# A depthwise convolution of 31 taps: 17 taps as band matrices over four tokens x 32 channels on TensorE, 14 taps on VectorE

## The chip, the cores and the metric

The kernel runs on one core of a Trainium2 chip. The metric is the device time of one execution in microseconds (us). A core has five engines that each work through an instruction list of their own, in order: TensorE (PE in the profile; its weight loads are shown apart, as PEld), VectorE (DVE), ScalarE (ACT), GpSimd (POOL) and SyncE (SP), which here only issues DMA transfers. They meet at semaphores. Matmuls read SBUF and write PSUM; DVE and ACT reach both memories.

## What is computed

The model has two layers on 512 tokens of width 1024: a mixer with a feed-forward part, then a conformer convolution with a feed-forward part. The change lies in the conformer:

```python
def conformer_conv(t, w1, b1, dw_w, dw_b, ln_g, ln_b, w2, b2):
    a, gate = jnp.split(t @ w1 + b1, 2, axis=-1)
    u = dwconv1d(a * jax.nn.sigmoid(gate), dw_w, dw_b)
    u = jax.nn.silu(layer_norm(u, ln_g, ln_b))
    return u @ w2 + b2
```

`dwconv1d` is a convolution along the tokens, each channel with its own 31 weights: out[t] is the sum over d from -15 to 15 of w[d] u[t+d], with zeros outside. All in float32.

## The kernel before

Data lies with channels on the 128 partitions and the 512 tokens along the free axis, so the 1024 channels are eight blocks `i` of 128. Every product in float32 is made of three matmuls: both factors are split into a rounded high part and the rest (type fp32r), and `mm3w` (lines 214 to 216) issues high x high, high x low and low x high into one PSUM tile. The projections `ps` of `cw1` and `cw2` go that way, 8 x 3 matmuls of 512 columns for one block of output. Weights come by DMA as `wraw`, ACT casts them to `whi`, POOL or DVE subtracts to `wlo` (`_wload`).

The conformer works through the blocks in four pairs, `ip` = 0, 2, 4, 6. For each block PE projects gate and value, ACT takes the sigmoid `sg` (line 1128), and DVE makes `u` (line 1133), which lies in PSUM for blocks 0 to 5 and in SBUF for 6 and 7. `split` (lines 985 and 986) gives `uhi` on ACT and `ulo` on DVE. The convolution is then shared out:

- ACT does the centre tap and the bias into the accumulator `cr` (line 1146).
- PE does 10, 10, 12 and 20 taps per block in the four pairs (`PE_TAPS`), each as a product with a diagonal matrix: `diag` scales the identity by the 128 weights on ACT, once for the high and once for the low part (lines 1109 and 1110, 208 instructions in all), and `mm3w` sums into `pc`. A tap is a shifted slice of `uhi` and `ulo`.
- DVE does the others, 20, 20, 18 and 10 per block, one fused multiply-add each over all tokens (`ve`, line 1163), by turns on the accumulators of the two blocks of the pair.

`add` brings both together on DVE (line 1168) and adds to the sums for the layer norm, `a1` and `a2` (`ln_add`, lines 929 to 931: a square on ACT, two additions, on POOL for the first three pairs and on DVE for the last). The last pair is done in two halves of 256 tokens. `stats_later` hangs two callbacks into `mm3w` that fire after a count of products: the first sums over partitions on PE (`sm`, line 945) and runs 15 tiny DVE operations to the mean `st` and the inverse deviation `rs`; the second spreads these on PE (`pb`, line 961) and starts `normed`, which is 24 DVE operations a half (lines 966, 967 and 986) with the Silu on ACT (line 1116) between them. Then `group("cw2")` projects (`psg`), the first half of the tokens first; `flush` in it fires the callbacks that are still open.

A scheduler orders each engine's list by the program's order and its own view of when things are ready; waits come from the tiles' dependencies.

Of the kernel before, what the change touches and what calls it, by code (L numbers as in the profile page):

```python
# [147 lines left out]
class Net:  # L148
# [62 lines left out]
    def mm3w(self, ps, w, a, start, stop):  # L211
# [4 lines left out]
        mm(ps, w[1], a[0], start=False, stop=stop)  # L216
# [870 lines left out]
    def conformer(self):  # L1087
        nc = self.nc
        PAD = 16
# [13 lines left out]
        kept = {}

        def diag(i, tap, bufs=4):
            wc = slice(tap * 8 + i, tap * 8 + i + 1)
            dhi = ct.tile([P, P], F32R, tag=f"dhi{bufs}", name="dhi", bufs=bufs)
            dlo = ct.tile([P, P], F32R, tag=f"dlo{bufs}", name="dlo", bufs=bufs)
            nc.scalar.mul(dhi, self.ident, whi[:, wc].bitcast(F32))
            nc.scalar.mul(dlo, self.ident, wlo[:, wc].bitcast(F32))  # L1110
            return dhi, dlo
# [10 lines left out]
        for ip in range(0, KT, 2):  # L1122
            us = []
            for i in (ip, ip + 1):
                pg = nxt(D + i * P)
                pa = nxt(i * P)
                sg = self.work.tile([P, T], F32, tag="t", name="sg")
                nc.scalar.activation(out=sg, in_=pg, func=AF.Sigmoid, bias=self.pc("cb1", 8 + i))
# [4 lines left out]
                nc.vector.scalar_tensor_tensor(out=u, in0=pa, scalar=self.pc("cb1", i), in1=sg, op0=ALU.add, op1=ALU.mult)
# [8 lines left out]
            pet = self.PE_TAPS[ip // 2]
            mid = KC // 2
            pcs = [self.mm.tile([P, T], F32, tag="mm", name="pc") for _ in us]
            for i, (u, _, _) in zip((ip, ip + 1), us):
                nc.scalar.activation(out=cr[:, i, :], in_=u, func=AF.Identity, scale=self.pc("cdw", mid * 8 + i), bias=self.pc("cdb", i))  # L1146
# [108 lines left out]
```

## Time and profile before

| | |
|---|---|
| median of 3 runs | 1750.29 us (1748.7 to 1751.08) |
| profiled execution | 1750.37 us, span 1748.6 us |
| conformer's convolution, first `pc` to first normalise operation of the second half | 1163.17 to 1316.91 |

The page gives the engines' busy time as a share of the span, and the chain of work that ended last. Rows of a timeline give start, duration, engine, line, operation and output <- inputs, with shapes; idle time of the engine ahead of a row stands in brackets with what ended it. Durations of matmuls overlap: what one costs is the step from start to start.

### The profile page before, as it was taken

What the parts mean: (1) busy time and instruction counts of PE and PEld (TensorE: products, weight loads), DVE (VectorE), ACT (ScalarE), POOL (GpSimd) and SP (SyncE); (2) the same over time, 40 slices, a digit from 0 to 9 for tenths busy, and PEclk for the clock granted to TensorE, in tenths of its full rate; (3) what the DMA queues carried; (4) which work ended last, traced back from release to release, by engine and by line L of the source; (5) the groups of instructions that cost most, each with busy time, mean ns of one, the idle gap of its engine ahead of it and who ended that gap; (6) DMA issues with size and microseconds to landing.
All of it is one profiled execution on the core that took longest, in us unless ns stands there. A gap on an engine that the chain in (4) does not pass through costs nothing.

```text
span 1748.6 us, 26467 instructions
## 1 busy us (share of the span) xinstructions
PE 1700.7 (97%) x9574; PEld 1459.9 (83%) x9574; DVE 1244.6 (71%) x2386; ACT 850.4 (49%) x1713; POOL 518.2 (30%) x428
## 2 busy tenths in 40 slices
PE   6999999999999999999999999999999899999996
PEld 4987778989999898788888888978899788888886
DVE  6778988979696894678777741488788877776125
ACT  4556775444444453355434322399635743333223
POOL 4400000000000001545444444533415344444452
PEclk9999999999999999999999999999999999999998
DMA  9721102444444334634334343321103333333332
GB/s 363 237 73 49 31 19 89 145 135 156 133 145 131 97 105 150 218 87 131 111 110 122 110 134 96 109 73 61 56 31 91 85 96 97 97 97 97 97 99 76
DMA packets 92193, 194.02 MB, mean 111 GB/s; under 512 B 10496, under 2 KB 13568, under 8 KB 92064
## 3 DMA queue, kind: packets, MB, share of 16 engines
q1 hardware_dynamic: 92016, 192.21, 35.3%
q8 instruction: 75, 1.23, 0.3%
q14 instruction: 54, 0.44, 0.1%
q0 software_dynamic: 48, 0.13, 0.0%
HBM read 190.21 MB, written 2.10 MB: 110 GB/s over the span
## 4 chain that ended last, share of the span: by engine, by line
PE 88%; DVE 6%; ACT 2%; DMA 1%; issue 1%; POOL 0%; SPq 0%; DVEq 0%; POOLq 0%; ACTq 0%
PE ps L214 18%; PE ps L216 18%; PE ps L215 18%; PE lev L744 3%; PE psz L234 2%; PE psz L233 2%; PE psz L235 2%; PE psh L214 2%; PE psh L216 2%; PE psh L215 2%; PE seg L645 2%; PE psv L234 1%; PE psv L235 1%; PE psv L233 1%; PE psg L215 1%; PE pc L215 1%
## 5 line engine op out<-in xcount | busy, mean ns | idle before, releaser
L188 POOL TENSOR_TENSOR wlo<-wraw,whi 128x512 fp32r<-128x512 f32 x380 | 502.4, 1327 | 1183.6 <-ACT whi L184 1164.0
L184 ACT CAST whi<-wraw 128x512 fp32r<-128x512 f32 x488 | 300.8, 619 | 496.6 <-PE ps L215 247.6
L214 PE MATMUL ps<-h1hi,whi 128*128 128x512 f32 x768 | 299.0, 389 | 0.8 <-DVE acc L1071 0.8
L216 PE MATMUL ps<-h1hi,wlo 128*128 128x512 f32 x768 | 299.2, 390 | 0.5 <-POOL wlo L188 0.5
L215 PE MATMUL ps<-h1lo,whi 128*128 128x512 f32 x768 | 298.9, 389 | 0.0
L1071 DVE SCALAR_TENSOR_TENSOR acc<-ps,pcol,acc 128x441 f32<-128x441 f32 (+2 forms) x320 | 222.4, 695 | 57.2 <-ACT acc L1063 47.7
L216 PEld LDWEIGHTS ps<-h1hi,wlo 128*128 128x128 f32 x768 | 144.2, 188 | 31.4 <-POOL wlo L188 1.8
L214 PEld LDWEIGHTS ps<-h1hi,whi 128*128 128x128 f32 x768 | 144.2, 188 | 31.1 <-issue 1.6
L215 PEld LDWEIGHTS ps<-h1lo,whi 128*128 128x128 f32 x768 | 144.2, 188 | 29.3
L273 DVE CUSTOM_DVE_ANT_0 junk<-ada,sc,pcol 128x1024 bf16<-128x1024 f32 x80 | 108.3, 1354 | 15.8 <-DMA ada<-adaw 15.5
L909 DVE SCALAR_TENSOR_TENSOR x<-ps,mod,x 128x512 f32<-128x512 f32 x14 | 10.5, 751 | 141.6 <-PE ps L216 141.6
L188 DVE TENSOR_TENSOR wlo<-wraw,whi 128x512 fp32r<-128x512 f32 x108 | 73.8, 689 | 42.7 <-ACT whi L184 42.3
L214 PE MATMUL ps<-ghi,whi 128*128 128x512 f32 x264 | 102.7, 389 | 0.0
L215 PE MATMUL ps<-glo,whi 128*128 128x512 f32 x264 | 102.7, 389 | 0.0
L216 PE MATMUL ps<-ghi,wlo 128*128 128x512 f32 x264 | 102.7, 389 | 0.0
L1163 DVE SCALAR_TENSOR_TENSOR cr<-u,pcol,cr 128x511 f32<-128x511 f32 (+20 forms) x156 | 98.0, 705 | 1.4 <-ACT cr L1146 1.2
L214 PE MATMUL ps<-hhi,whi 128*128 128x512 f32 x240 | 97.9, 408 | 0.0
L215 PE MATMUL ps<-hlo,whi 128*128 128x512 f32 x240 | 96.7, 403 | 0.0
L216 PE MATMUL ps<-hhi,wlo 128*128 128x512 f32 x240 | 96.2, 401 | 0.0
L986 DVE TENSOR_TENSOR glo<-acc,ghi 128x512 fp32r<-128x512 f32 x44 | 55.8, 1268 | 28.2 <-ACT ghi L985 28.0
L233 PE MATMUL psz<-whi,hhi 128*128 128x256 f32 (+1 forms) x224 | 67.6, 302 | 0.0
L234 PE MATMUL psz<-wlo,hhi 128*128 128x256 f32 (+1 forms) x224 | 67.5, 301 | 0.0
(355 smaller groups left out, 4145.9 us busy)
## 6 DMA issues: line engine op xcount, KB each, us to landing
wraw<-wst SPq DMA_DIRECT2D x488, 256.0 KB, 2.7
ada<-adaw SPq DMA_DIRECT2D x104, 512.0 KB, 3.6
xk<-xT SPq DMA_DIRECT2D x8, 256.0 KB, 7.8
x<-xT SPq DMA_DIRECT2D x8, 256.0 KB, 4.4
out<-n SPq DMA_DIRECT2D x16, 128.0 KB, 1.7
xk<-ctxT SPq DMA_DIRECT2D x8, 128.0 KB, 4.0
sc<-rows SPq DMA_DIRECT2D x1, 512.0 KB, 3.5
scc<-rows SPq DMA_DIRECT2D x1, 512.0 KB, 8.4
```

What stands on the lines that cost most here:

```text
L184: nc.scalar.copy(hi, raw)
L188: eng.tensor_tensor(out=lo, in0=raw, in1=hi.bitcast(F32), op=ALU.subtract)
L214: mm(ps, w[0], a[0], start=start, stop=False)
L215: mm(ps, w[0], a[1], start=False, stop=False)
L216: mm(ps, w[1], a[0], start=False, stop=stop)
L233: mm(ps, a[0], w[0], start=start, stop=False)
L234: mm(ps, a[0], w[1], start=False, stop=False)
L235: mm(ps, a[1], w[0], start=False, stop=stop)
L273: nc.vector.tensor_tensor_reduce(out=junk, in0=raw, in1=self.sc if cond is None else cond, scale=1.0, scalar=self.pc("adab", n), op0=ALU.m ...
L986: return nc.vector.tensor_tensor(out=lo, in0=x, in1=hi.bitcast(F32), op=ALU.subtract)
L1071: nc.vector.scalar_tensor_tensor(out=o, in0=grid(pg)[:, r0 + dy - 1:r1 + dy - 1, c0 + dx - 1:c1 + dx - 1], scalar=wcol(dy, dx), in1=o, op0 ...
L1163: nc.vector.scalar_tensor_tensor(out=acc[:, t0:t1], in0=u[:, t0 + d:t1 + d], scalar=self.pc("cdw", tap * 8 + i), in1=acc[:, t0:t1], op0=AL ...
```

## The change

The 17 middle taps (d = -8 to 8, the centre apart, which stays on ACT) go to PE for all eight blocks, in another layout, and the 14 outer ones to DVE.

With token t = 4m + q, the partitions hold four phases q x 32 channels instead of 128 channels, and the free axis the 128 values of m, for four groups g of 32 channels. A matrix of 128x128 then takes all 4 x 4 combinations of input and output phase at one shift of m. Five shifts (-2 to 2) and four groups, 20 matrices a block, do the 17 taps. They are laid out on the host as the new input `band`; `bands` loads them (four DMAs of 128x640 a block on SP), splits them on ACT (`bhi`) and POOL (`blo`). A matrix takes two matmuls: the high part by the high and low parts of u side by side (256 columns, line 1147) and the low part by the high part (128 columns, line 1148).

`phases` brings u there: a copy on ACT that puts the phases side by side (`up`), a DMA from ACT's queue to HBM (`ud`), four from SP's queue back (`uw`, runs of 512 bytes), a cast on ACT and a subtraction on DVE into `uhl`. `conv` brings the result back: two copies on ACT (`ct`) and two additions on DVE (`cv`, line 1152) put the two column halves together, a DMA writes to HBM (`vd`), four read it back with channels on the partitions (`cb`, line 1157), and DVE adds it to `cr` (line 1160). All of `vd` and `cb` are on SP's queue.

`conv` of block i-1 is issued behind the projections of block i; those of blocks 6 and 7 come in the two halves, at the end. `ve` has one block and one accumulator now. `ln_add` is on DVE throughout. `tick` is the callback count, taken out of `mm3w`.

```diff
+        def bands(i):
+            out = []
+            for g in range(PH):
+                raw = ct.tile([P, NS * P], F32, tag="braw", name="braw")
+                nc.sync.dma_start(out=raw, in_=self.A["band"][i * PH + g])
...
+                nc.scalar.copy(hi, raw)
+                nc.gpsimd.tensor_tensor(out=lo, in0=raw, in1=hi.bitcast(F32), op=ALU.subtract)
...
+        def phases(u):
+            up = ct.tile([P, PH, P], F32, tag="pv", name="up", bufs=4)
+            nc.scalar.copy(up, u[:].rearrange("p (m q) -> p q m", q=PH))
+            d = dp.tile([P, T], F32, tag="ud", name="ud")
+            nc.scalar.dma_start(out=d, in_=up)
...
+            for q in range(PH):
+                nc.sync.dma_start(out=w[q * CB:(q + 1) * CB, :, 2:P + 2],
+                                  in_=d[:, q * P:(q + 1) * P].rearrange("(g c) m -> c g m", g=PH))
...
+            nc.scalar.copy(hl[:, :, 0, :], w)
+            nc.vector.tensor_tensor(out=hl[:, :, 1, :], in0=w, in1=hl[:, :, 0, :].bitcast(F32), op=ALU.subtract)
+            return hl
+        def conv(i, hl, bm, h0, h1):
+            m0, n = h0 // PH, (h1 - h0) // PH
...
+                    for k, sh in enumerate(SH):
+                        o = 2 + sh + m0
+                        nc.tensor.matmul(pc[:, g - gg, :, :], hi[:, k * P:(k + 1) * P], hl[:, g, :, o:o + n], start=k == 0, stop=False)
+                        nc.tensor.matmul(pc[:, g - gg, 0, :], lo[:, k * P:(k + 1) * P], hl[:, g, 0, o:o + n], start=False, stop=k == NS - 1)
+                        self.tick()
+                t = self.work.tile([P, 2, n], F32, tag="t", name="ct")
+                nc.scalar.copy(t, pc[:, :, 1, :])
+                nc.vector.tensor_tensor(out=v[:, gg:gg + 2, 0:n], in0=pc[:, :, 0, :], in1=t, op=ALU.add)
+            d = dp.tile([P, PH * n], F32, tag=f"vd{n}", name="vd")
+            nc.sync.dma_start(out=d, in_=v[:, :, 0:n])
+            b = self.work.tile([P, PH, P], F32, tag="t", name="cb")
+            for g in range(PH):
+                nc.sync.dma_start(out=b[g * CB:(g + 1) * CB, :, 0:n],
+                                  in_=d[:, g * n:(g + 1) * n].rearrange("(q c) m -> c q m", q=PH))
...
+            nc.vector.tensor_tensor(out=acc, in0=acc, in1=b[:, :, 0:n], op=ALU.add)
...
+        for i in range(KT):
...
+            hl = phases(u)
...
+            if i < KT - 1:
+                for j, *ops in before:
+                    conv(j, *ops, 0, T)
+                    self.ln_add(ln, j, cr[:, j, :], 0, T)
+                before = []
+                ve(i, u, 0, T)
+            before.append((i, hl, bands(i)))
...
+        for half in HALVES:
+            ve(KT - 1, u, *half)
+        for half in HALVES:
+            for j, *ops in before:
+                conv(j, *ops, *half)
+            for j, *_ in before:
+                self.ln_add(ln, j, cr[:, j, :], *half)
+            self.stats_later(ln, *half, 7, 9, lambda p, half=half: normed(*half, p))
```

The first place is PE's list where the convolution begins, in the changed kernel: the last projection matmuls of block 1 (`ps`), then the first matrices of block 0 (`pc`).

```order
L217 MATMUL ps<-h1hi,whi_11399 128x512
L218 MATMUL ps<-h1lo,whi_11399 128x512
L219 MATMUL ps<-h1hi,wlo_11401 128x512
L1147 MATMUL pc<-uhl,bhi 128x256
L1148 MATMUL pc<-uhl,blo 128x128
```

Before, the diagonal products `pc<-uhi,dhi` of block 0 stood there; now `uhl` is awaited at the same place. The second place is DVE's list from the first `u`, in the changed kernel: the taps of blocks 0 and 1 (line 1178), the second `u` and the first subtraction for `uhl` (line 1134).

```order
L1191 SCALAR_TENSOR_TENSOR u<-psg,pcol,sg 128x512
L1178 SCALAR_TENSOR_TENSOR cr<-u,pcol,cr 128x497
L1178 SCALAR_TENSOR_TENSOR cr<-u,pcol,cr 128x498
L1191 SCALAR_TENSOR_TENSOR u<-ps,pcol,sg 128x512
L1178 SCALAR_TENSOR_TENSOR cr<-u,pcol,cr 128x499
L1178 SCALAR_TENSOR_TENSOR cr<-u,pcol,cr 128x500
L1178 SCALAR_TENSOR_TENSOR cr<-u,pcol,cr 128x497
...
L1178 SCALAR_TENSOR_TENSOR cr<-u,pcol,cr 128x503
L1178 SCALAR_TENSOR_TENSOR cr<-u,pcol,cr 128x500
L1134 TENSOR_TENSOR uhl<-uw,uhl 128x4x132
```

Ten taps and the second `u` stand ahead of the subtraction. The third place is DVE's list in the last pair. Before: the additions of `pc` of the second half (line 1168) among the normalise operations of the first half (lines 966, 967 and 986).

```order
L966 TENSOR_TENSOR n<-cr,pb 128x256
L1168 TENSOR_TENSOR cr<-cr,pc 128x256
L967 TENSOR_TENSOR n<-n,pb 128x256
...
L966 TENSOR_TENSOR n<-cr,pb 128x256
L1168 TENSOR_TENSOR cr<-cr,pc 128x256
L986 TENSOR_TENSOR h1lo<-n,h1hi 128x256
```

In the changed kernel, from the last normalise operations of the first half (lines 972, 973 and 992) on:

```order
L972 TENSOR_TENSOR n<-cr,pb 128x256
L973 TENSOR_TENSOR n<-n,pb 128x256
L992 TENSOR_TENSOR h1lo<-n,h1hi 128x256
L1152 TENSOR_TENSOR cv<-pc,ct 128x2x64
L992 TENSOR_TENSOR h1lo<-n,h1hi 128x256
L1152 TENSOR_TENSOR cv<-pc,ct 128x2x64 x2
L1160 TENSOR_TENSOR cr<-cr,cb 128x4x64
L936 TENSOR_TENSOR a_11383<-a_11383,cr 128x256
L937 TENSOR_TENSOR a_11384<-a_11384,sq 128x256
L1160 TENSOR_TENSOR cr<-cr,cb 128x4x64
```

Three of the four `cv` of the second half, which its `vd` waits for, have moved behind the first half's normalise operations. SyncE's list there alternates, for both halves alike:

```order
L1154 DMA vd<-cv 512x1x64
L1157 DMA cb<-vd 32x4x64 x4
L1154 DMA vd<-cv 512x1x64
L1157 DMA cb<-vd 32x4x64 x4
```

A write of one block stands behind the four reads of the block ahead of it, which wait for that block's write.

More of the change, by code (lines that the diff above doesn't have):

```diff
@@ L35 @@
 KC = 31
+PH, CB = 4, P // 4
+SH = (-2, -1, 0, 1, 2)
+BAND = (PH * SH[0], PH * SH[-1])
 C_Z = 0
@@ L1102, in conformer @@
         nxt = lambda c: ready.pop(0) if ready else self.fm(self.mm, "cw1", c, self.act)
[L1103 to L1111, printed above, removed]
+        NS = len(SH)
@@ new lines, in bands @@
+        def bands(i):
[3 more added lines that the diff above has]
+                nc.sync.dma_start(out=raw, in_=self.A["band"][i * PH + g])
+                hi = ct.tile([P, NS * P], F32R, tag="bhi", name="bhi", bufs=8)
+                lo = ct.tile([P, NS * P], F32R, tag="blo", name="blo", bufs=8)
+                nc.scalar.copy(hi, raw)
+                nc.gpsimd.tensor_tensor(out=lo, in0=raw, in1=hi.bitcast(F32), op=ALU.subtract)
+                out.append((hi, lo))
+            return out
@@ new lines, in ve @@
+        def ve(i, u, h0, h1):
+            acc = cr[:, i, :]
+            for d in range(-(KC // 2), KC // 2 + 1):
+                if BAND[0] <= d <= BAND[1]:
+                    continue
+                t0, t1 = max(h0, -d), min(h1, T - d)
+                nc.vector.scalar_tensor_tensor(out=acc[:, t0:t1], in0=u[:, t0 + d:t1 + d], scalar=self.pc("cdw", (d + KC // 2) * 8 + i),
+                                               in1=acc[:, t0:t1], op0=ALU.mult, op1=ALU.add)
+        before = []
+        for i in range(KT):
+            pg = nxt(D + i * P)
+            pa = nxt(i * P)
+            sg = self.work.tile([P, T], F32, tag="t", name="sg")
+            nc.scalar.activation(out=sg, in_=pg, func=AF.Sigmoid, bias=self.pc("cb1", 8 + i))
+            if i < KT - 2:
+                u = self.lnps.tile([P, T], F32, tag="pb", name="u", bufs=2)
+            else:
+                u = ct.tile([P, T], F32, tag="u", name="u")
+            nc.vector.scalar_tensor_tensor(out=u, in0=pa, scalar=self.pc("cb1", i), in1=sg, op0=ALU.add, op1=ALU.mult)
+            hl = phases(u)
+            nc.scalar.activation(out=cr[:, i, :], in_=u, func=AF.Identity, scale=self.pc("cdw", KC // 2 * 8 + i), bias=self.pc("cdb", i))
+            if i % 2:
+                self.next_x(i // 2)
+            if i < KT - 1:
+                for j, *ops in before:
+                    conv(j, *ops, 0, T)
+                    self.ln_add(ln, j, cr[:, j, :], 0, T)
+                before = []
+                ve(i, u, 0, T)
+            before.append((i, hl, bands(i)))
@@ L1235, in layout @@
     out["rows"] = np.concatenate([f["c"][0], f["c_ctx"], f["ssd_dt_bias"][0].ravel(), f["ssd_a_log"][0].ravel(), f["ssd_d"][0]])[None]
+    w = f["conf_dw_w"][0].reshape(KC, KT * PH, CB)
+    band = np.zeros((KT * PH, PH, CB, len(SH), PH, CB), np.float32)
+    c = np.arange(CB)
+    for a in range(PH):
+        for k, sh in enumerate(SH):
+            for b in range(PH):
+                d = PH * sh + a - b
+                if d and BAND[0] <= d <= BAND[1]:
+                    band[:, a, c, k, b, c] = w[d + KC // 2]
+    out["band"] = band.reshape(KT * PH, P, len(SH) * P)
     s, t = np.arange(P)[:, None], np.arange(P)[None, :]
```

86 lines of the change are left out of this document (15 added, 71 removed).

## The prediction

> **What bounds the kernel now.** I read the busy shares, then the chain of waits, then a table of stretches through the conformer, then single rows of PE and DVE at the table's gaps.
>
> ```profile
> PE 1700.7 (97%) x9574; PEld 1459.9 (83%) x9574; DVE 1244.6 (71%) x2386; ACT 850.4 (49%) x1713; POOL 518.2 (30%) x428
> PE 88%; DVE 6%; ACT 2%; DMA 1%; issue 1%; POOL 0%; SPq 0%; DVEq 0%; POOLq 0%; ACTq 0%
> ...
> 1163.00:1190.00 27.00, 26.76 (x116) 21.54 (x115) 26.40 (x41) 26.94 (x82) 8.05 (x15) 1.00 0.20 56
> 1190.00:1214.00 24.00, 23.77 (x103) 19.06 (x103) 18.03 (x28) 23.96 (x68) 8.71 (x11) 1.00 0.17 59
> 1214.00:1240.00 26.00, 26.00 (x116) 21.38 (x115) 20.40 (x33) 20.20 (x51) 15.61 (x16) 1.00 0.26 74
> 1270.00:1285.00 15.00, 15.00 (x110) 14.21 (x109) 15.00 (x27) 4.31 (x7) 5.14 (x4) 1.00 0.23 71
> 1285.00:1311.00 26.00, 23.99 (x190) 23.78 (x189) 20.20 (x64) 8.49 (x19) 0.00 (x0) 0.93 0.00 1
> ```
>
> The lines from the third on are a stretch and its length, then busy time of PE, PEld, DVE, ACT and POOL, the granted clock, the DMA share and GB/s. PE bounds the kernel, also in the convolution: it works 26.76 of 27 us and 15.00 of 15. But in the first and fourth of these stretches DVE is full too (26.40 of 27, 15.00 of 15). Work taken from PE is therefore worth its length only where DVE gives time as well. Three rows of PE fix the stage:
>
> ```profile
> 1163.17 0.49 PE L214 MATMUL pc<-uhi,dhi 128*128 128x512 f32 x1
> 1274.47 0.28 PE L214 MATMUL pc<-uhi,dhi 128*128 128x256 f32 x1
> 1290.96 0.39 PE L214 MATMUL pc<-uhi,dhi 128*128 128x256 f32 x1 [2.01 <-DVE cr L1168]
> ```
>
> The convolution starts at 1163.17, the projections are over at 1274.47, and the one wait of 2.01 us is PE waiting for DVE.
>
> **PE: what goes and comes.** Steps between starts (the first two rows are four matmuls apart, the other pairs one):
>
> ```profile
> 1273.33 0.39 PE L215 MATMUL ps<-h1lo,whi 128*128 128x512 f32 x1
> ...
> 1274.23 0.40 PE L216 MATMUL ps<-h1hi,wlo 128*128 128x512 f32 x1
> ...
> 1212.66 0.40 PE L214 MATMUL pc<-uhi,dhi 128*128 128x512 f32 x1
> 1212.90 0.40 PE L215 MATMUL pc<-ulo,dhi 128*128 128x512 f32 x1
> ...
> 1283.78 0.28 PE L214 MATMUL pc<-uhi,dhi 128*128 128x256 f32 x1
> 1283.90 0.28 PE L215 MATMUL pc<-ulo,dhi 128*128 128x256 f32 x1
> ...
> 313.46 1.05 PE L744 MATMUL lev<-kq,kg 128*128 128x128 f32 x8
> ```
>
> A projection matmul costs 0.225 us, a diagonal one of 512 columns 0.24, one of 256 columns 0.12. Eight of 128 columns take 1.05, so with 0.28 for the last, as at 256 columns, (1.05 - 0.28)/7 = 0.11 each: halving the columns once more brings almost nothing. Before: 192 x 0.24 + 240 x 0.12 = 75 us. After: six blocks of 20 pairs at 0.12 + 0.11, 27.6; the last two blocks in halves, 160 x 0.11 = 17.6; together 45. **PE is relieved of 30 us.** A block then holds PE for two projections and a convolution, 48 x 0.225 + 4.6 = 15.4 us. No row shows a matmul of this type (fp32 in its rounded form) under 256 columns; its bounds are 0.11 and the 0.225 of a 512-column one. I take 0.11, from the row of the same size, and keep the other for a rival.
>
> **The start.** PE's order puts the convolution of block 0 right behind the projections of block 1, which end at 1163.1. It needs `uhl`, the regrouped data.
>
> ```profile
> 1161.63 0.76 DVE L1133 SCALAR_TENSOR_TENSOR u<-psg,pcol,sg 128x512 f32<-128x512 f32 x1 [2.42 <-ACT sg L1128]
> ...
> 1163.75 0.75 DVE L1133 SCALAR_TENSOR_TENSOR u<-ps,pcol,sg 128x512 f32<-128x512 f32 x1
> 1164.92 0.75 DVE L1163 SCALAR_TENSOR_TENSOR cr<-u,pcol,cr 128x507 f32<-128x507 f32 x1 [0.42 <-ACT cr L1146]
> ...
> 1166.18 24.32 DVE L1163 SCALAR_TENSOR_TENSOR cr<-u,pcol,cr 128x508 f32<-128x508 f32 x37
> 1191.00 1.52 DVE L1163 SCALAR_TENSOR_TENSOR cr<-u,pcol,cr 128x498 f32<-128x498 f32 x2
> ...
> wraw<-wst SPq DMA_DIRECT2D x488, 256.0 KB, 2.7
> out<-n SPq DMA_DIRECT2D x16, 128.0 KB, 1.7
> xk<-ctxT SPq DMA_DIRECT2D x8, 128.0 KB, 4.0
> ```
>
> The data's way: u ends at 1162.4, a copy on ACT (0.6, as the cast of 590 ns below), a write to HBM, a read back as four transfers, a cast (0.6), a subtraction on DVE. A DMA of 128 KB lands 1.7 us (the output) to 4.0 us (the context) after its issue, one of 256 KB after 2.7; I take 2.5 for every one. The queue spends about 0.33 us on each issue (row below). So 1162.4 + 0.6 + 2.5 + 3 x 0.33 + 2.5 + 0.6 = 1169.6. DVE's order has ten taps ahead of the subtraction: 37 alternating taps took 24.32, about 0.66 each, two successive ones on one accumulator 1.52, so a tap that waits for the one ahead of it costs 0.775. Ten at 0.66 to 0.775 from 1164.9, then 0.6: 1172.1 to 1173.3. The later one decides: PE stands about 9.7 us from 1163.1, where it waited for almost nothing.
>
> **DVE from the start to the last u.** VectorE loses 30 of 156 taps, but the 14 of a block share one accumulator.
>
> ```profile
> L986 DVE TENSOR_TENSOR glo<-acc,ghi 128x512 fp32r<-128x512 f32 x44 | 55.8, 1268 | 28.2 <-ACT ghi L985 28.0
> L188 POOL TENSOR_TENSOR wlo<-wraw,whi 128x512 fp32r<-128x512 f32 x380 | 502.4, 1327 | 1183.6 <-ACT whi L184 1164.0
> ...
> L986 DVE TENSOR_TENSOR ulo<-u,uhi 128x512 fp32r<-128x512 f32 x8 | 5.7, 711 | 4.6 <-ACT uhi L985 3.1 <-POOL a L930 1.5
> L985 ACT CAST uhi<-u 128x512 fp32r<-128x512 f32 x8 | 4.7, 590 | 5.1 <-DVE u L1133 5.1
> ...
> 1190.40 0.69 DVE L1168 TENSOR_TENSOR cr<-cr,pc 128x512 f32<-128x512 f32 x1
> ...
> 1301.25 0.42 DVE L1168 TENSOR_TENSOR cr<-cr,pc 128x256 f32<-128x256 f32 x1
> 1301.59 0.41 DVE L967 TENSOR_TENSOR n<-n,pb 128x256 f32<-128x256 f32 x1
> ```
>
> Between the first tap and u(7) stand 98 taps: the 28 of the first two blocks alternate, 18.5 us; 70 on one accumulator, 54.3. Six u at 0.66, 4.0. Twelve additions `cv` of 256 columns at 0.34, 4.1. Behind most u DVE waits for the centre tap on ACT: 1163.75 to 1164.92 is 1.17, 0.5 more than u itself, and the new copy of u stands ahead of it (0.6): five times 1.1, 5.5. Then 23 operations with two operands in SBUF (seven subtractions, six additions of `cb`, ten of the layer norm, which leave POOL for DVE). Alone one costs 0.6 (from 1190.40 to the next tap at 1191.00); in the FFN, where POOL subtracts weights, the same form takes 1.27. POOL loses the norm's additions but gains four subtractions of 128x640 a block, 1.33 x 640/512 = 1.66: with four weight subtractions of 1.33 it is busy 12 us of a 16 us block. I take 1.27, the nearer row: 29.2, and keep 13.8. Sum 115.6: **u(7) at 1164.9 + 115.6 = 1280.5**; by 0.6 at 1265. PE's own pace, 1172.8 + 6 x 15.4 = 1265.2, is the floor. Before, u(7) stood here:
>
> ```profile
> 1279.41 0.74 DVE L1133 SCALAR_TENSOR_TENSOR u<-ps,pcol,sg 128x512 f32<-128x512 f32 x1
> ...
> 1281.52 9.06 DVE L1163 SCALAR_TENSOR_TENSOR cr<-u,pcol,cr 128x256 f32<-128x256 f32 x23
> ...
> 1311.25 0.42 DVE L931 TENSOR_TENSOR a<-a,sq 128x256 f32<-128x256 f32 x1
> 1313.03 0.16 DVE L948 TENSOR_SCALAR st<-sm 128x4 f32<-128x4 f32 x1 [1.36 <-PE sm L945]
> ...
> 1316.91 0.42 DVE L966 TENSOR_TENSOR n<-cr,pb 128x256 f32<-128x256 f32 x1 [0.77 <-PE pb L961]
> ...
> L1023 SPq DMA_DIRECT2D out<-n x16: 332/332/348, 1726.0 to 1745.5; - x16
> ```
>
> So the 30 us saved on PE have gone to the start and to DVE when the tail begins.
>
> What stays beside it: ACT loses 208 diagonal builds and gains some 5 us of casts and copies a block, and has room (20.20 of 26 us busy in 1214 to 1240 even with the builds). The 10.5 MB of matrices add some 90 GB/s over 120 us where the stretches show 56 to 71 and a DMA share of 0.2. If POOL fell behind its 12 in 16 us, PE would wait for `blo`.
>
> **The tail.** From u(7): u 0.66 and the wait 1.1, 1282.3. 28 half taps at 0.394 (9.06 for 23) with the subtraction among them, 11.6, and the last `cv` of block 6: 1293.9. Conv(7) of this half (40 x 0.11, behind the subtraction after 20 taps) ends at 1295.3. Now SyncE alone carries the result: write block 6, wait, read it as four transfers, write block 7, wait, read. Only then DVE may add. With L for a landing that is 3L + 4 x 0.33 + 3 x 0.33 = 9.8 us at L = 2.5 (7.4 at 1.7, 14.3 at 4.0), to 1303.7. Block 7's `cv` is ready about 1296, but its write stands behind block 6's reads, at 1297.7. Addition, square, sum: 1.4, estimated from three 0.42 operations and their hand-overs. Sums to first normalise operation: 1311.67 to 1316.91 before, 5.2. Half 0 starts to normalise at 1310.3. In DVE's order three of the four `cv` of half 1 stand behind all of half 0's 24 normalise operations (before, the second half's additions stood among them): 24 x 0.44 = 10.6 us (an estimate: 0.42 each and a little for hand-overs), and 0.6 for `cv`: 1321.5. Then again 9.8 + 1.4 + 5.2: **half 1 is normalised from 1337.9, where it was 1316.91: +21.0.** What follows is as before. PE's matmuls between have nothing to do then; its clock falls after waits:
>
> ```profile
> 1293.13 0.41 PE L216 MATMUL pc<-uhi,dlo 128*128 128x256 f32 x1
> 1293.34 0.41 PE L214 MATMUL pc<-uhi,dhi 128*128 128x256 f32 x1
> ```
>
> After the 2.01 us wait a step is 0.21 for some 3.4 us instead of 0.12, a loss of 1.5. One such loss in a place that counts: 1.5. Sum +22.5 on the profiled run of 1750.4 (span 1748.6 and 1.8 around it; the median of the runs is 1750.3): **1773**.
>
> The tail's four reads have runs of 256 bytes, those of the other blocks 512. No row here shows such a transfer by itself, so 1.7 and 4.0 are the bounds. The Trainium skill (DMA: Bandwidth & Descriptors, Specifications) says that under 512 bytes the DMA engines read, modify and write and do not reach line rate; by that the tail's reads land late, as in the second rival.
>
> **The rivals.**
> - DVE keeps PE's pace: its two-operand additions cost 0.6, because POOL's instructions fall elsewhere. From a mean of about 0.6 the floor of 1265.2 decides: u(7) 15.3 earlier, and with L = 1.7 in both halves 4.8 more: 1753, **not slower** by the measure below. For it: before, the eight subtractions beside the taps took 0.71. Against it: POOL was 8 of 27 us busy then.
> - Long landings: L = 4.0 adds 4.5 in each half, 1782. For it: many small runs; against it: 1.7 for the output.
> - Matmuls under 256 columns cost 0.23: a block holds PE 48 x 0.225 + 20 x 0.345 = 17.7 us, u(7) 1279 nearly as by DVE, and conv(7) of half 0 40 x 0.115 longer: 1778. Against it: the 0.11 row.
> - The PE saving survives whole: half 1's trip is covered and only the start is paid: 1750.4 - 30 + 9.7 = 1730. Against it: DVE's order.
>
> **How the numbers follow.** Forecast 0.60 (1764 to 1781), long landings 0.14, narrow matmuls 0.10, DVE keeping pace 0.11, saving survives 0.05. The low bound is the first rival's 1753 without the loss of clock, 1751; the high one has long landings and narrow matmuls together, 1787, and some for waits that I didn't count: 1791. A measurement tells 0.2% (3.5 us) from no change. Faster: the last rival and a little of the first, 0.07; same: most of the first, 0.08; slower the rest.
>
> **What would show it.** PE idle about 10 us ahead of the first `pc`; DVE full from 1164 to u(7), with its `cr` additions near 1.27; u(7) within 5 us of 1280; two gaps of about 10 us between the last `cv` and the additions of `cb` in the tail; normalising of half 1 some 21 us later. Wrong it is if DVE has idle time in the steady blocks, or if `cb` is there when DVE comes to it.

## The result, and the profile after

| | before | forecast | after |
|---|---|---|---|
| median of 4 runs, us | 1750.68 (1748.7 to 1753.52) | 1773 (1751 to 1791) | 1795.45 (1793.96 to 1795.81) |
| first `pc` on PE | 1163.17 | 1172.8 | 1174.51 |
| last `u` on DVE, u(7) | 1279.41 | 1280.5 | 1294.79 |
| first half normalised from | 1300.89 | 1310.3 | 1335.18 |
| second half normalised from | 1316.91 | 1337.9 | 1360.89 |

The ratio is 1.0254, with a 95% interval of 1.024 to 1.0267: slower, as forecast, by twice as much as forecast. The profiled execution took 1795.75 us, its span 1794.0. The miss of 23.0 at the last mark has three parts: 14.3 up to u(7), 10.6 from there to the first half's normalise operations, and -1.9 from half to half.

The busy shares and the chain that ended last, of the changed kernel:

```profile
PE 1706.6 (95%) x9542; PEld 1473.6 (82%) x9542; DVE 1257.6 (70%) x2385; ACT 819.2 (46%) x1564; POOL 555.1 (31%) x434
PE 82%; DVE 8%; DMA 3%; ACT 3%; issue 1%; SPq 1%; POOL 0%; DVEq 0%; ACTq 0%; POOLq 0%
```

PE is busy for 6 us more, though it was to be relieved of 30. The table of stretches (columns as in the prediction) says why:

```profile
1163.00:1190.00 27.00, 17.42 (x87) 15.26 (x86) 22.97 (x36) 16.57 (x28) 16.69 (x16) 0.81 0.61 185
1285.00:1311.00 26.00, 12.71 (x59) 12.61 (x59) 22.37 (x42) 5.35 (x9) 4.01 (x5) 0.56 0.23 71
1311.00:1330.00 19.00, 19.00 (x91) 19.00 (x91) 3.64 (x9) 1.52 (x5) 0.00 (x0) 0.50 0.12 28
```

At the start PE works 17.42 of 27 us, where it was full. From 1311 to 1330 it is 100% busy with 91 matmuls, at a granted clock of 0.50, and DVE has 3.64 us of work. A full PE is no PE at its peak here. PE waits five times for regrouped data, 31.2 us in all; the three longest waits, from its timeline:

```profile
1174.51 0.58 PE L1147 MATMUL pc<-uhl,bhi 128*128 128x256 f32 x1 [9.58 <-DVE uhl L1134]
1289.17 0.48 PE L1147 MATMUL pc<-uhl,bhi 128*128 128x128 f32 x1 [5.54 <-DVE uhl L1134]
1307.03 0.44 PE L1147 MATMUL pc<-uhl,bhi 128*128 128x128 f32 x1 [9.12 <-DVE uhl L1134]
```

They wait for the data of block 0, block 6 and block 7. DVE's timeline shows where its time went:

```profile
1193.33 1.10 DVE L1160 TENSOR_TENSOR cr<-cr,cb 128x512 f32<-128x512 f32 x1 [4.94 <-DMA cb<-vd]
...
1279.36 9.14 DVE L1178 SCALAR_TENSOR_TENSOR cr<-u,pcol,cr 128x501 f32<-128x501 f32 x8
...
1321.94 0.62 DVE L1160 TENSOR_TENSOR cr<-cr,cb 128x256 f32<-128x256 f32 x1 [4.03 <-DMA cb<-vd]
...
1323.11 0.42 DVE L937 TENSOR_TENSOR a<-a,sq 128x256 f32<-128x256 f32 x1
...
1330.45 0.16 DVE L954 TENSOR_SCALAR st<-sm 128x4 f32<-128x4 f32 x1 [6.71 <-PE sm L951]
...
1335.18 0.42 DVE L972 TENSOR_TENSOR n<-cr,pb 128x256 f32<-128x256 f32 x1 [1.84 <-PE pc L1148]
```

Three things were not in the sum. Five of the six additions before u(7) wait for `cb`, 11.1 us in all; the first of these waits, 4.94, stands behind the stop at the start, the others belong to the blocks in the middle. The taps of block 6, whose u lies in SBUF, take 9.14/8 = 1.14 each in the mean and not 0.775. And after the last addition of the first half (1323.11) DVE waits 6.71 us for the sums `sm` from PE. The experiments take these apart, with the stop at the start.

### The profile page after: what moved, and what is told of

It is laid out like the page before. It is cut to its first block, busy times and chain, and to the rows that moved or that the text cites. A ratio compares the mean times of both kernels' runs of the same rounds, so it can differ in the third digit from the quotient of the medians.

```text
span 1794.0 us, 26479 instructions
## 1 busy us (share of the span) xinstructions
PE 1706.6 (95%) x9542; PEld 1473.6 (82%) x9542; DVE 1257.6 (70%) x2385; ACT 819.2 (46%) x1564; POOL 555.1 (31%) x434
## 3 DMA queue, kind: packets, MB, share of 16 engines
q10 hardware_dynamic: 1152, 2.10, 0.3%
## 4 chain that ended last, share of the span: by engine, by line
PE 82%; DVE 8%; DMA 3%; ACT 3%; issue 1%; SPq 1%; POOL 0%; DVEq 0%; ACTq 0%; POOLq 0%
PE ps L217 17%; PE ps L219 17%; PE ps L218 16%; PE lev L750 3%; DVE cr L1178 2%; PE psz L240 2%; PE psz L241 2%; PE psz L239 2%; PE seg L651 2%; PE psh L217 2%; PE psh L219 2%; PE psh L218 2%; DMA ada<-adaw 1%; PE psv L240 1%; PE psv L241 1%
## 5 line engine op out<-in xcount | busy, mean ns | idle before, releaser
L279 DVE CUSTOM_DVE_ANT_0 junk<-ada,sc,pcol 128x1024 bf16<-128x1024 f32 x80 | 107.1, 1338 | 17.6 <-DMA ada<-adaw 17.5
L1147 PE MATMUL pc<-uhl,bhi 128*128 128x256 f32 (+1 forms) x200 | 70.7, 421 | 31.2 <-DVE uhl L1134 31.2
L1178 DVE SCALAR_TENSOR_TENSOR cr<-u,pcol,cr 128x498 f32<-128x498 f32 (+14 forms) x126 | 88.2, 726 | 13.7 <-ACT cr L1193 11.7
L1147 PEld LDWEIGHTS pc<-uhl,bhi 128*128 128x128 f32 x200 | 55.0, 275 | 33.1 <-DVE uhl L1134 23.8
```

Of the source, the lines that this page charges most:

```text
L279: nc.vector.tensor_tensor_reduce(out=junk, in0=raw, in1=self.sc if cond is None else cond, scale=1.0, scalar=self.pc("adab", n), op0=ALU.m ...
L1147: nc.tensor.matmul(pc[:, g - gg, :, :], hi[:, k * P:(k + 1) * P], hl[:, g, :, o:o + n], start=k == 0, stop=False)
L1178: nc.vector.scalar_tensor_tensor(out=acc[:, t0:t1], in0=u[:, t0 + d:t1 + d], scalar=self.pc("cdw", (d + KC // 2) * 8 + i), in1=acc[:, t0:t ...
```

## The experiments

In the table, ratios are to the kernel before, timed in the same job, so the changed kernel stands at 1.0254 [1.024, 1.0267]. "Against the change" is the difference of the two ratios times 1752.5, the kernel before in these jobs. The three columns on the right are from the one profiled execution of each: a block of the middle (u(2) to u(6), divided by four), u(7) to the first normalise operation of half 0, and from that to the one of half 1.

| run | edit | median us | ratio [95%] | against the change | block | u(7) to half 0 | to half 1 |
|---|---|---|---|---|---|---|---|
| the change | | 1795.45 | 1.0254 [1.024, 1.0267] | | 19.1 | 40.4 | 25.7 |
| e1_wide | wide matmuls in the tail | 1790.14 | 1.0211 [1.0196, 1.0227] | -7.5 | 19.0 | 33.3 | 25.7 |
| e8_mid96 | half-wide ones | 1792.33 | 1.0226 [1.0209, 1.0243] | -4.9 | 19.3 | 34.6 | 25.6 |
| e11_flush | sums ahead of half 1 on PE | 1794.17 | 1.0238 [1.0223, 1.0253] | -2.8 | 19.3 | 34.6 | 28.6 |
| e2_vdfirst | both writes ahead of the reads | 1793.5 | 1.0242 [1.0224, 1.0259] | -2.1 | 19.2 | 40.6 | 23.4 |
| e6_fulltail | tail in one trip a block | 1777.51 | 1.0142 [1.0122, 1.0163] | -19.6 | 19.4 | 33.0 | 14.6 |
| e12_nostart | block 0 waits for nothing | 1787.78 | 1.0202 [1.0185, 1.0219] | -9.1 | 19.0 | 40.4 | 25.5 |
| e3_late | addition a block later | 1792.75 | 1.0229 [1.0214, 1.0244] | -4.4 | 18.2 | 40.6 | 25.6 |
| e4_upsum | u of 6 and 7 in PSUM | 1787.67 | 1.0200 [1.0185, 1.0216] | -9.5 | 19.4 | 38.0 | 25.6 |
| e5_bloonce | a quarter of the low parts | 1783.81 | 1.0179 [1.0159, 1.0199] | -13.1 | 17.3 | 40.9 | 25.6 |
| e9_braw4 | e4, four raw buffers | 1780.58 | 1.0162 [1.0147, 1.0177] | -16.1 | 17.5 | 38.0 | 25.6 |
| e13_sporder | weight loads behind `cb` on SP | 1796.64 | 1.0253 [1.0236, 1.027] | -0.2 | 19.7 | 41.9 | 25.6 |
| e7_combo | e6, e3 and e4 | 1765.24 | 1.0071 [1.0055, 1.0087] | -32.1 | 18.2 | 31.7 | 14.3 |
| e10_best | e7, three raw buffers, tap first | 1764.24 | 1.0066 [1.0051, 1.0081] | -32.9 | 17.3 | 31.7 | 14.1 |

### Is it the clock that makes the tail long?

e1 gives the tail's matmuls the width of the other blocks, 256 and 128 columns, twice as many as are used:

```diff
-                pc = self.mm.tile([P, 2, 2, n], F32, tag="mm", name="pc")
+                pc = self.mm.tile([P, 2, 2, P], F32, tag="mm", name="pc")
...
-                        nc.tensor.matmul(pc[:, g - gg, :, :], hi[:, k * P:(k + 1) * P], hl[:, g, :, o:o + n], start=k == 0, stop=False)
+                        nc.tensor.matmul(pc[:, g - gg, :, :], hi[:, k * P:(k + 1) * P], hl[:, g, :, o:o + P], start=k == 0, stop=False)
```

> Blocks 6 and 7 compute all 128 columns of m in each half and use 64 of them: the same 160 matmuls, but 256 and 128 columns wide instead of 128 and 64. Theory A (the clock is granted by how much of the time columns stream, and 192 columns in a pair of 0.4255 us are too few): in the tail the clock comes back to 1.00 within about 4 us of each start, a pair falls from 0.4255 to 0.23 us although it has twice the columns, and the first normalise operations come 8 to 10 us earlier: 1784 to 1788 us. Rival B (the clock stays low for another reason, such as the gap ahead, or a pair costs its two weight loads at any clock): pairs stay at 0.43 us, 1795 us. Rival C (columns cost time at a low clock): slower than 1795 us.

Stretches of 4 us in the tail, first of the changed kernel, then of e1:

```profile
1310.00:1314.00 4.00, 4.00 (x21) 4.00 (x21) 0.29 (x1) 0.27 (x1) 0.00 (x0) 0.50 0.19 46
1314.00:1318.00 4.00, 4.00 (x21) 4.00 (x20) 1.67 (x4) 0.68 (x2) 0.00 (x0) 0.50 0.17 40
```

```profile
1310.00:1314.00 4.00, 4.00 (x25) 4.00 (x25) 0.74 (x3) 0.27 (x1) 0.00 (x0) 0.63 0.16 40
1314.00:1318.00 4.00, 4.00 (x37) 4.00 (x36) 1.76 (x4) 0.68 (x2) 0.00 (x0) 1.00 0.24 58
```

Twice the columns, and done sooner: PE's clock, at half since its wait until 1307.48, rises between 1310 and 1314 (0.63 is a mean) and stays at 1.00 until 1323; a pair then takes 0.23 us, and half 0 is normalised 7.1 us sooner after u(7). The order of PE's list is nearly the same: the sums of half 0 stand behind 374 of the `pc` matmuls in e1 and behind 379 in the changed kernel. A pair with the narrow columns stays at 0.43, from PE's timeline of the changed kernel:

```profile
1313.85 0.45 PE L1147 MATMUL pc<-uhl,bhi 128*128 128x128 f32 x1
...
1314.28 0.45 PE L1147 MATMUL pc<-uhl,bhi 128*128 128x128 f32 x1
```

So the slow clock behind the wait of 9.12 us cost far more than the 1.5 us that the prediction allowed: 7.5 us by the times. e8 asks whether the width decides, with 192 and 96 columns:

```diff
+            nw = P if n == P else 96
+            f0 = 0 if m0 == 0 else P - nw
```

> As the experiment with doubled columns, but 192 and 96 columns a pair in the tail instead of 256 and 128 (96 of the 128 values of m are computed in each half, 64 are used). It asks where the clock comes back: if 288 columns in about 0.43 us are enough, the tail runs at 1.00 after some 4 us as with 384, and the time is 7 us under that of the changed kernel, 1788 to 1791 us; if not, it stays at 0.50 as with 192, 1794 to 1797 us.

```profile
1318.00:1322.00 4.00, 4.00 (x20) 4.00 (x20) 1.60 (x4) 0.68 (x2) 0.00 (x0) 0.50 0.16 39
```

The clock stays at 0.50, with a pair at 0.43. Half 0 comes 5.8 us sooner after u(7) all the same, by another cause: in e8's PE list the sums of half 0 stand behind 357 of the 400 `pc` matmuls, in the changed kernel behind 379, and the next run moves just that. Of the three widths, 192 and 288 columns per pair kept the half clock and 384 released it. Why is not shown.

The long wait is not needed for it. In e9 (below) PE waits only 0.98 us ahead of block 6's narrow pairs and begins them at full clock, at 0.22 us a pair. After 2.8 us of them the clock falls to half, though PE is busy all the time:

```profile
1276.60:1279.40 2.80, 2.80 (x25) 2.80 (x26) 2.69 (x4) 0.00 (x0) 2.64 (x4) 1.00 0.69 205
1279.60:1282.40 2.80, 2.80 (x15) 2.80 (x15) 2.77 (x4) 1.84 (x3) 0.00 (x0) 0.50 0.52 170
```

In e10 (below), where the pairs at this place are wide, a longer wait of 2.31 us ahead of them left the clock at 1.00 until they were done.

### The order of the tail

The sums of half 0 stand behind 59 of half 1's 80 matmuls on PE, at 0.43 for two. e11 puts them ahead of all 80:

```diff
+            with self.tc.issue_after(self.summed.ins) if half is HALVES[1] else nullcontext():
...
+            if half is HALVES[0]:
+                self.flush()
```

> The sums of the first half stand in TensorE's list ahead of the second half's 80 matmuls instead of behind 59 of them. Theory A (the first half's normalising waited for these matmuls at half clock, 11.7 us from the last addition to the first normalise operation instead of 5.2): the first half is normalised about 6 us earlier; the second half's 80 matmuls now end 17 us after the sums, about when they are needed: 4 to 6 us in all, a ratio of 1.022 to 1.023. Rival B (the second half waits for its matmuls as long as the first one gains): 1.025.

DVE's timeline of e11:

```profile
1326.04 0.16 DVE L954 TENSOR_SCALAR st<-sm 128x4 f32<-128x4 f32 x1 [1.46 <-PE sm L951]
...
1330.56 0.42 DVE L972 TENSOR_TENSOR n<-cr,pb 128x256 f32<-128x256 f32 x1 [1.62 <-PE pb L967]
```

The wait for `sm` falls from 6.71 to 1.46 us and half 0 comes 5.8 sooner after u(7). Half 1, whose matmuls now begin later, takes 2.9 back: it had used the time. The 2.8 us that the times show can't be told from no gain by the intervals alone.

e2 issues both writes of a half ahead of any read of it:

```diff
-            for j, *ops in before:
-                conv(j, *ops, *half)
+            ds = [(j, conv(j, *ops, *half)) for j, *ops in before]
+            with self.tc.issue_after(self.wrote.ins):
+                for j, d in ds:
+                    back(j, d, *half)
```

> In each half both writes to HBM are issued ahead of the eight reads, where block 7's write stood behind block 6's reads. Theory (SyncE's order is what spaces the two additions of a half, 5.6 us in half 0 and 4.2 in half 1): the second half's last addition comes 2 to 3 us earlier, the first half's also, but there TensorE's order hides it: 1792 to 1794 us. Rival (the writes of block 7 are late anyway because its products are): first half as it was, second half 1 to 2.5 us: 1793 to 1795 us.

The two additions of half 1 now stand 1.85 us apart (4.17 in the changed kernel), and half 1 comes 2.3 us sooner after half 0; the times, 2.1 us apart, can't tell it from no gain by their intervals. That half 0 gained nothing has its reason in SP's timeline of the changed kernel:

```profile
1310.03 0.59 SPq L1154 DMA_DIRECT2D vd<-cv  x1
1312.39 1.73 SPq L1157 DMA_DIRECT2D cb<-vd  x4
1316.44 0.52 SPq L1154 DMA_DIRECT2D vd<-cv  x1
1318.72 1.73 SPq L1157 DMA_DIRECT2D cb<-vd  x4
```

The second write starts 2.3 us after the last read was issued (1312.39 + 1.73 = 1314.12). It is not queued behind the reads; it waits for block 7's products, which PE makes at half clock.

e6 computes blocks 6 and 7 at their whole width, one write and one read each; only the additions are in halves:

```diff
+        d6, d7 = [(conv(j, *ops, 0, T)) for j, *ops in before]
...
+        put(KT - 2, back(KT - 2, d6, 0, T), 0, T)
+        self.ln_add(ln, KT - 2, cr[:, KT - 2, :], 0, T)
+        b7 = back(KT - 1, d7, 0, T)
+        for half in HALVES:
+            put(KT - 1, b7, *half)
```

> Blocks 6 and 7 are convolved once over all tokens instead of in two halves (80 matmuls of 256 and 128 columns instead of 160 of 128 and 64), with one return trip each; block 6's lies beside block 7's taps, and both halves are added up before the first is normalised. Theory A (the halves cost their doubled weight loads at half clock, and a second trip behind the first half's normalising): the second half is normalised about 12 us behind the first instead of 25.7, the first about as late or some us earlier; 1773 to 1779 us. Rival B (the trip and the cold start of TensorE set the tail, whatever is halved): 1787 to 1794 us.

It is the largest single gain, 19.6 us. u(7) to half 0 is 7.4 us shorter: these matmuls are wide, as in e1, and no other products stand ahead of the sums. Half 1 follows 14.6 us later and not 25.7: its data is there when DVE comes to it. So the second trip through HBM, with its products, cost 11.1 us. The gain of the whole run is that of one trip and of wide matmuls together.

### The start

e12 gives the matrices of block 0 zeros in place of the regrouped u, so they wait for nothing; 17 taps of block 0 are left out of the result by that, and block 0's way through HBM with its subtraction of 0.7 us on DVE:

```diff
+        zero = ct.tile([P, PH, 2, P + 4], F32R, tag="uhl", name="zero", bufs=3)
...
-            hl = phases(u)
+            hl = phases(u) if i else zero
```

> Block 0's matrices take zeros that lie in SBUF from the start (17 taps of block 0 are left out), so that TensorE does not wait 9.6 us for the first way through HBM. Theory A (DVE sets the pace up to u(7), and the stop at the start costs only what DVE has to wait for later, 4.9 us for the first return and a fall of the clock): DVE also loses a subtraction of 0.7 us; 3 to 6 us in all, 1.022 to 1.0235. Rival B (the stop at the start is paid in full): 9 to 10 us, 1.020.

PE's timeline of e12, the last projection matmul and the first matmul of the convolution:

```profile
1165.13 0.40 PE L219 MATMUL ps<-h1hi,wlo 128*128 128x512 f32 x1
1165.37 0.28 PE L1147 MATMUL pc<-zero,bhi 128*128 128x256 f32 x1
```

The stop is gone and 9.1 us with it, nearly all of the 9.58. From u(0) to u(2) it is 23.0 us and not 30.8. Nothing later covers the start.

### What sets the pace of the blocks in the middle?

The addition of a block waits for `cb`. The chain of waits of the changed kernel, followed through one block, looks like a closed loop:

```profile
1239.07 2.41 DMA uw<-ud
...
1241.54 0.63 ACT uhl L1133
1242.18 0.53 ACT whi L187
1242.74 1.14 POOL wlo L191
1243.89 0.35 SPq L185
...
1244.29 0.60 SPq L1112
...
1244.99 0.38 SPq L1157
...
1246.36 2.78 DMA cb<-vd
...
1249.27 1.11 DVE cr L1160
...
1250.94 0.68 ACT sg L1186
...
1251.68 0.77 DVE u L1191
```

Regrouped data of the next block lands; a cast of weights stands behind its cast on ACT; POOL's subtraction frees a weight buffer; a weight load and a band load on SP, queued ahead of the reads, go out; only then the reads of `cb` (L1157). The write `vd` had been issued at 1239.60, 5.4 us before the reads, and such a write lands in 2.4. The addition stands ahead of the next u on DVE, and so on. Which link is the cause? Four runs break one each.

e3 breaks DVE's: the addition comes one block later, behind the seventh tap.

```diff
+                if d == -9:
+                    with self.tc.issue_after(tap.ins):
+                        for j, b in todo:
+                            put(j, b, 0, T)
+                            self.ln_add(ln, j, cr[:, j, :], 0, T)
```

> The addition of the returned result of a block and its two layer-norm additions are moved behind the seventh tap of the next block but one, so that DVE does not wait for the read from HBM (five waits, 11.1 us in all before u(7)). Theory A (DVE sets the pace of the steady blocks, and these waits are on its path): u(7) comes 8 to 11 us earlier and the kernel takes 1784 to 1788 us. Rival B (TensorE or the way of u through HBM sets the pace, and the waits fill with others): 1793 to 1796 us.

DVE's groups between 1190 and 1300 (count, then busy time and mean ns of one, then idle time ahead of them), first of the changed kernel, then of e3:

```profile
L1160 DVE TENSOR_TENSOR cr<-cr,cb 128x512 f32<-128x512 f32 x6 | 7.7, 1283 | 11.1 <-DMA cb<-vd 11.1
L1134 DVE TENSOR_TENSOR uhl<-uw,uhl 128x528 fp32r<-128x528 f32 x5 | 4.8, 968 | 0.0
```

```profile
L1170 DVE TENSOR_TENSOR cr<-cr,cb 128x512 f32<-128x512 f32 x6 | 9.8, 1634 | 0.0
L1134 DVE TENSOR_TENSOR uhl<-uw,uhl 128x528 fp32r<-128x528 f32 x5 | 7.0, 1397 | 0.0
```

All 11.1 us of waits for `cb` are gone, yet a block is only 0.9 us shorter, and from the first tap to u(7) it is 3.4 us less. The same eleven operations take 16.8 us and not 12.5: 4.3 of the 11.1 came back as longer instructions. Another 5.1 came back as one wait for PE's projection of block 2, which stands in PE's list behind the stop at the start:

```profile
1192.22 0.76 DVE L1207 SCALAR_TENSOR_TENSOR u<-ps,pcol,sg 128x512 f32<-128x512 f32 x1 [5.09 <-PE ps L219]
```

ACT waited for raw matrices as long as before (23.5 us, 21.2 in the changed kernel).

e13 breaks SP's order: weight loads go behind the reads.

```diff
-            pg = nxt(D + i * P)
-            pa = nxt(i * P)
+            with self.tc.issue_after(self.read.ins) if i > 1 else nullcontext():
+                pg = nxt(D + i * P)
+                pa = nxt(i * P)
```

> The weight loads of a block are issued on SP behind the reads of cb of two blocks before, so that a read of cb no longer stands behind a load that waits for POOL's subtraction; nothing is computed otherwise. Theory A (SP's list holds the reads back on a closed loop u - HBM - convolution - HBM - next u, which sets the period of 19 us): the issue of vd and that of cb come within 1 to 2 us of each other in place of 5.4, the waits of the addition for cb fall from 11 us to under 4 us before the last u, that u ends 5 to 10 us earlier, ratio 1.020 to 1.0225. Rival B (the time is given back by DVE beside POOL and by weights that now come late, as when the addition alone was moved): waits move to the matrices' or the weights' loads, the last u is within 3 us of where it was, ratio 1.024 to 1.026.

SP's timeline of e13, then a row of its table of waits (total, times, longest):

```profile
1241.44 0.38 SPq L1154 DMA_DIRECT2D vd<-cv  x1
1241.91 2.79 SPq L1112 DMA_DIRECT2D braw<-band  x2
1244.75 1.99 SPq L1157 DMA_DIRECT2D cb<-vd  x4
```

```profile
ACT bhi L1115 <- DMA braw<-band: 32.3, 12, 4.5
```

Rival B: nothing gained. The weight load is out of the way, and two band loads take its place ahead of the reads: 3.3 us from write to read. The waits for `cb` before u(7) fall from 11.1 to 8.1, those of ACT for raw matrices rise from 21.2 to 32.3. So the place of the weight loads alone is not the cause.

e5 takes work from POOL: low parts are computed for blocks 0 and 1 only and used again, so 24 of 32 subtractions of 128x640 are left out, and six blocks get low parts that belong to other channels.

```diff
+                if i < 2:
+                    lo = ct.tile([P, NS * P], F32R, tag="blo", name="blo", bufs=8)
+                    nc.gpsimd.tensor_tensor(out=lo, in0=raw, in1=hi.bitcast(F32), op=ALU.subtract)
+                    los.append(lo)
+                else:
+                    lo = los[i % 2 * PH + g]
```

> The low parts of the band matrices are made for blocks 0 and 1 only and used again for the others (24 subtractions of 1.57 us on GpSimd are left out, so the output is off by the low parts of the weights). Theory A (GpSimd's subtractions stretch DVE's operations with two SBUF operands): the additions of cb fall from 1.1 to about 0.7 us, block 6's taps from 16.6 to 11 to 14 us, u(7) comes 4 to 8 us earlier, 1789 to 1792 us. Rival B (these are slow through DMA or PSUM traffic): no change, 1795 to 1797 us.

A block falls to 17.3 us, and the time by 13.1. POOL was busy only some 11.5 of 19 us, so it isn't full; what matters is what waits for it. e4 and e9 show that. e4 first moves u of blocks 6 and 7 to PSUM:

```diff
-            if i < KT - 2:
+            if i < KT:
```

> u of blocks 6 and 7 lies in PSUM as that of the others does, instead of SBUF. Theory A (block 6's 14 taps took 16.6 us instead of 10.9 because they read two operands from SBUF while GpSimd works): they fall to about 11 us, u(7) comes 5 to 6 us earlier, 1789 to 1791 us. Rival B (they were slow through the wait for each other or for DMA): 1794 to 1796 us.

DVE's timeline of e4 in block 6:

```profile
1279.73 5.39 DVE L1178 SCALAR_TENSOR_TENSOR cr<-u,pcol,cr 128x501 f32<-128x501 f32 x7
...
1291.04 0.75 DVE L1191 SCALAR_TENSOR_TENSOR u<-ps,pcol,sg 128x512 f32<-128x512 f32 x1
```

A tap takes 5.39/7 = 0.77, where it took 1.14, and u(6) to u(7) falls from 24.0 to 17.8. The 1.14 is a mean of two prices. Two stretches of the changed kernel inside block 6's taps, three taps each:

```profile
1280.89:1286.17 5.28, 2.74 (x13) 1.92 (x11) 5.20 (x3) 2.25 (x5) 4.74 (x3) 1.00 0.19 64
1286.21:1288.40 2.19, 0.00 (x0) 0.00 (x0) 2.12 (x3) 0.00 (x0) 0.00 (x0) 0.99 0.72 190
```

While POOL subtracts (4.74 of 5.28 us) a tap takes 5.28/3 = 1.76 us, and 2.19/3 = 0.73 while it is idle; e4's taps, with u in PSUM, take their 0.77 beside POOL's subtractions. The Trainium skill (SBUF — State Buffer, Who interferes with whom) has DVE share its second pair of SBUF ports with GpSimd, under an exclusive lock. These prices agree with it.

e9 is e4 with four buffers for the raw matrices in place of two:

```diff
-                raw = ct.tile([P, NS * P], F32, tag="braw", name="braw")
+                raw = ct.tile([P, NS * P], F32, tag="braw", name="braw", bufs=4)
```

> u of blocks 6 and 7 in PSUM as in the experiment on that, and the raw band matrices have four buffers instead of two. Theory A (with two buffers the load of a matrix waits until GpSimd has subtracted the one before the last; ScalarE's cast then waits for the load, and the copies ct and casts that stand behind it in ScalarE's list wait with it, then DVE): against u in PSUM alone (a ratio to the kernel before of 1.020) 4 to 7 us less, 1.016 to 1.018, ScalarE's waits for the matrices (21 us in the changed kernel) fall under 8. Rival B (GpSimd's subtractions hurt only by stretching DVE's operations): no change, 1.019 to 1.021.

Against e4, one number has changed. In e4 the table of waits has this row; e9's has none for `braw`:

```profile
ACT bhi L1115 <- DMA braw<-band: 22.9, 12, 3.8
```

SP's timeline of e9 around the same block:

```profile
1238.30 0.38 SPq L1154 DMA_DIRECT2D vd<-cv  x1
1240.28 0.35 SPq L185 DMA_DIRECT2D wraw<-wst  x1
1240.68 0.43 SPq L1112 DMA_DIRECT2D braw<-band  x1
1241.20 2.28 SPq L1157 DMA_DIRECT2D cb<-vd  x4
```

The reads follow the write by 2.9 us, about its landing, though both loads still stand between. A block takes 17.5 us where e4 had 19.4, and the time falls by a further 6.7; the intervals of e4 and e9 don't meet. So the pace was set by the preparation of the matrices: with two raw buffers, a load waits until ACT and POOL are done with an earlier one, and all that stands behind it on SP, `cb` with it, waits too. ACT's list passes the delay on as well, since its copies `ct` stand behind casts that wait for raw matrices: from e4 to e9 DVE's waits before u(7) fall from 12.2 to 6.4 us for `cb` and from 3.7 to nothing for `ct`. No run separates the two lists. Relieving POOL (e5) or adding buffers (e9) shortens a block by 1.8 to 1.9 us; reordering a list shortens it by 0.9 (e3) or not at all (e13).

### Is there a version that beats both?

e7 has the edits of e6, e3 and e4 together. e10 adds a third raw buffer and puts the centre tap ahead of the copy of u on ACT.

```diff
-                raw = ct.tile([P, NS * P], F32, tag="braw", name="braw")
+                raw = ct.tile([P, NS * P], F32, tag="braw", name="braw", bufs=3)
...
-            hl = phases(u)
...
+            hl = phases(u)
```

> The whole-width tail together with the late addition and u in PSUM for all blocks. If the three gains add (20, 4 and 9 us): 1763 to 1768 us. If u in PSUM and the late addition overlap, or the tail takes back what u(7) gains: 1768 to 1775 us. Faster than the kernel before (1750 us) by none of the theories.

> The combination (whole-width tail, late addition, u in PSUM) with three buffers for the raw matrices, and with the centre tap ahead of the copy of u on ScalarE. If the two waits they take away (for matrices, and 0.6 us a block ahead of the first tap) are on DVE's path: 4 to 8 us under the combination, a ratio of 1.002 to 1.005 to the kernel before. If DVE's own work is the bound: 1.006 to 1.008. Not under 0.998 by either.

No. The three gains of e7 add up, 32.1 against 19.6 + 4.4 + 9.5 = 33.5. e10 adds nothing that can be told (the intervals meet): a block falls to 17.3 us, but the last u comes only 1.4 us sooner than in e7, at 1283.69. Both are still slower than the kernel before, by 0.7%. What is left to the kernel before, some 11.5 us, is close to the stop at the start; e7 without it was not tried.

## Why the prediction was right in sign and short in size

**The start: the length of the stop was right, but its cost was not in the sum.** 9.7 us were forecast and 9.58 measured, in part by luck: eleven taps stand ahead of the subtraction and not ten, so that it ends at 1174.5 and not at 1172.8, but the projections end later as well, at 1164.9 and not at 1163.1. In the forecast the stop only raises PE's floor of 1265.2, which lies under DVE's 1280.5, so it adds nothing to the time. That step failed: e12 shows that the stop is paid nearly in full, 9.1 us. DVE pays it as the first wait for `cb` (4.94), or, where that wait is taken away, as a wait for PE (5.1, e3).

**DVE up to u(7): the sum failed, 115.6 forecast and 129.1 measured from the first tap.** The step was "23 operations ... I take 1.27" for POOL's share of the trouble, with no wait for what comes back from HBM. The operations took 20.5 and not 29.2, so that term was 8.7 too high. Missing were waits for `cb` (11.1), waits of `cv` for `ct` (3.1), 5.7 of stretched taps in block 6 and 2.3 of waits for the centre tap. The prediction had a sentence on it, "if POOL fell behind its 12 in 16 us, PE would wait for `blo`", and had named as proof against itself that "`cb` is there when DVE comes to it"; the matrices' preparation did set the pace, yet not through PE, but through two buffers and the lists of SP and ACT (e9, e5). A block by the forecast's terms was 14 x 0.775 + 0.66 + 0.68 + 1.1 + 4 x 1.27 = 18.4 us, and 19.1 came: close, by the wrong terms. The price of 0.775 for a tap held only where u lies in PSUM or POOL is idle (e4).

**The tail, half 0: the step "Conv(7) of this half (40 x 0.11, behind the subtraction after 20 taps) ends at 1295.3" failed.** From u(7) to the last layer-norm addition it was 28.7 and not 24.6 us, since PE took 0.43 a pair; to the normalise operations it was 11.7 and not 5.2 from there, since the sums stood behind half 1's pairs. The "one such loss in a place that counts: 1.5" was the mis-sized term: making the matmuls wide gives 7.5 us back (e1). The gains of e1 and e11 overlap, as both shorten the wait for `sm`; no run has both.

**The tail, half 1: the mechanism was right.** 27.6 us from half to half were forecast and 25.7 measured; e6 shows that the trip is what they are made of.

**PE's 30 us: right that they wouldn't survive.** The pairs do cost what was forecast when the clock is whole, 0.23 for a wide one (e1) and 0.22 for a narrow one (e9); at half clock a pair costs 0.43 in either width (a wide one at the start, from 1175.00 to 1175.43).

**The rivals.** DVE keeping PE's pace fell: its operations were cheaper than forecast, though not at the 0.6 of this rival (20.5/23 = 0.89), and it waited besides. Long landings fell: writes of 128 KB landed in 2.2 us and the tail's reads, with runs of 256 bytes, in 1.8 (2.5 was taken; the reads of the other blocks, with runs of 512 bytes and twice the data, took 2.7 and 2.9 in the median). So the rule on transfers under 512 bytes that the prediction quotes from the Trainium skill (DMA: Bandwidth & Descriptors, Specifications) did not show as a later landing here. Narrow matmuls at the price of wide ones fell at full clock; their true price was the clock that they didn't bring back, and in e9 didn't hold. The range failed because these costs come together: each half-clock, queue and buffer was weighed alone, or not at all.

## What to carry to other kernels

Where a change sends data through HBM inside a loop, write the loop down with every queue and buffer that it passes, also those of loads that have nothing to do with it: a wait named after the returned data may be set by a buffer of something else, and giving that buffer more room tells it in one run. A relieved TensorE that then waits, or gets narrow matmuls, loses clock too, so price its work at the lower clock until a trace shows that it recovers. And where work is split into halves so that they overlap, each half pays its own latency: here one trip for the whole, with matmuls of the whole width, was 19.6 us better.

## What the runs showed of the hardware that was not expected

- PE stayed at a granted clock of 0.50 through 19 us (1311 to 1330) in which the profile has it busy all the time, with pairs of 192 columns; also with 288 (e8). With 384 columns, in the same place, it was at 1.00 some 6 us after the wait (e1). Pairs of 192 columns that began at 1.00, after a wait of 0.98 us, were at 0.50 2.8 us later (e9). The Trainium skill (TensorE: Matmul & The Clock Gate, Part 1: The HAM clock gate) gives a warm-up budget of about 3.4 us of time, whatever the number of matmuls. For these narrow ones the measurement differs.
- At half clock a pair took 0.43 us with 192, 288 or 384 columns, and at full clock 0.23 with 384 (e1) and 0.22 with 192 (e9): the columns were not what it spent its time on.
- A fused multiply-add on DVE with all operands in SBUF took 1.76 us in the mean while POOL subtracted and 0.73 while POOL was idle; with u in PSUM it took 0.77 beside POOL (e4).
